# Cutting the stores behind a stream of loads into rows that grow from 4 KB to 64 KB

## The chip, the cores and the metric

The kernel runs on one core of a Trainium2 chip. The metric is the device time of one execution in microseconds (us). All timed executions here are in the fast state or, for single looks, of unknown state on one core at a granted clock of 1.0.

## The reference

Two inputs of 1024 x 4096 float32; the result is the GELU, in its tanh form, of their product.

```python
def reference(x, y):
    z = x * y
    return (0.5 * z * (1 + np.tanh(np.sqrt(2 / np.pi) * (z + 0.044715 * z ** 3)))).astype(np.float32)
```

## The kernel before

Each of 128 partitions holds 32,768 elements (128 KB) of x. x stays in SBUF (the memory on which the multiply and the GELU work; the inputs and the result lie in HBM, where the page has 33.55 MB read and 16.78 MB written), y goes through a ring of 64 KB; product and GELU are written over x in place, and x is stored. The loads and stores all go through the sync engine's one DMA queue (the page's only one, q1, with all 50.33 MB). Below, what the change and the argument touch (cuts marked by `# ...`).

```python
X_LOADS = [(0, 16384), (16384, 32768)]
Y_LOADS = [(0, 16384, 0), (16384, 24576, 0), (24576, 32768, 8192)]
STEP = 4096
STORES = [(0, 16384), (16384, 32768)]
# ...
    _hoist(nc, [load_x(0).ins, load_y(0).ins])     # issued first of all
    load_x(1)
    for i in (1, 2):
        nc.sync.wait_ge(sem_mul, (Y_LOADS[i][1] - Y_LOADS[1][0]) // STEP)
        load_y(i)
# ... vector: 8 multiplies of 128 x 4096; scalar: 8 GELUs of 128 x 4096, one behind each
    for i, (a, b) in enumerate(STORES):
        nc.sync.wait_ge(sem_act, b // STEP)
        nc.sync.dma_start(out=out_r[:, a:b], in_=xs[:, a:b]).then_inc(sem_o[i], 16)
    for i in range(len(STORES)):
        nc.sync.wait_ge(sem_o[i], 16)
```

The order on the queue is x, y, x (64 KB rows, 8.39 MB each), y, y (32 KB rows, 4.19 MB each), store, store (64 KB rows, 8.39 MB each). Of a 128-partition transfer each of the 16 DMA engines carries 8 rows, then one 4-byte packet for the semaphore: for the 7 transfers the trace has 896 packets of a row and 112 of 4 bytes, 1,008 in all.

Of the kernel before, what the change touches and what calls it, by code (L numbers as in the profile page):

```python
# [1 line left out]

# [4 lines left out]


F32 = mybir.dt.float32
GELU = mybir.ActivationFunctionType.Gelu_apprx_tanh  # L10


X_LOADS = [(0, 16384), (16384, 32768)]

Y_LOADS = [(0, 16384, 0), (16384, 24576, 0), (24576, 32768, 8192)]
STEP = 4096
STORES = [(0, 16384), (16384, 32768)]
Y_RING = 16384


def _hoist(nc, issued):

    here = nc.cur_bb.bb.instructions
    first = nc.main_func.blocks[0].instructions
    for ins in issued:
        del here[next(k for k, i in enumerate(here) if i is ins or i.name == ins.name)]
    engine = issued[0].engine
    at = next(
        k
        for k, i in enumerate(first)  # L30
        if i.engine == engine and type(i).__name__ == "InstDrain"
    )
    first[at:at] = issued


@with_exitstack
def kernel(
    ctx: ExitStack,
    tc: tile.TileContext,
    x: bass.AP,  # L40
    y: bass.AP,
    out: bass.AP,
):
    nc = tc.nc
    P = nc.NUM_PARTITIONS

    x_r = x.flatten_outer_dims().rearrange("(p a) c -> p (a c)", p=P)
    y_r = y.flatten_outer_dims().rearrange("(p a) c -> p (a c)", p=P)
    out_r = out.flatten_outer_dims().rearrange("(p a) c -> p (a c)", p=P)
    total_f = x_r.shape[1]  # L50


    tc.close()
    tc.compile()  # L54

    xs = nc.alloc_sbuf_tensor("xs", [P, total_f], F32).ap()
    ys = nc.alloc_sbuf_tensor("ys", [P, Y_RING], F32).ap()
    sem_x = [nc.alloc_semaphore(f"sem_x{i}") for i in range(len(X_LOADS))]
    sem_y = [nc.alloc_semaphore(f"sem_y{i}") for i in range(len(Y_LOADS))]
    sem_o = [nc.alloc_semaphore(f"sem_o{i}") for i in range(len(STORES))]  # L60
    sem_mul = nc.alloc_semaphore("sem_mul")
    sem_act = nc.alloc_semaphore("sem_act")

    def load_x(i):
        a, b = X_LOADS[i]
        return nc.sync.dma_start(out=xs[:, a:b], in_=x_r[:, a:b]).then_inc(sem_x[i], 16)  # L66

    def load_y(i):
        a, b, r = Y_LOADS[i]
        return nc.sync.dma_start(  # L70
            out=ys[:, r : r + b - a], in_=y_r[:, a:b]
        ).then_inc(sem_y[i], 16)

    _hoist(nc, [load_x(0).ins, load_y(0).ins])
# [5 lines that stand above are left out]
    n = 0  # L80
    for i, (a, b, r) in enumerate(Y_LOADS):
        for j, (xa, xb) in enumerate(X_LOADS):
            if xa <= a < xb:
                nc.vector.wait_ge(sem_x[j], 16)
        nc.vector.wait_ge(sem_y[i], 16)  # L85
        for c in range(a, b, STEP):
            nc.vector.tensor_mul(  # L87
                out=xs[:, c : c + STEP],
                in0=xs[:, c : c + STEP],
                in1=ys[:, r + c - a : r + c - a + STEP],  # L90
            ).then_inc(sem_mul, 1)
            n += 1
            nc.scalar.wait_ge(sem_mul, n)
            nc.scalar.activation(  # L94
                out=xs[:, c : c + STEP], in_=xs[:, c : c + STEP], func=GELU
            ).then_inc(sem_act, 1)

    for i, (a, b) in enumerate(STORES):
        nc.sync.wait_ge(sem_act, b // STEP)
        nc.sync.dma_start(out=out_r[:, a:b], in_=xs[:, a:b]).then_inc(sem_o[i], 16)  # L100
    for i in range(len(STORES)):
        nc.sync.wait_ge(sem_o[i], 16)
    nums = sorted(s.num for s in [*sem_x, *sem_y, *sem_o, sem_mul, sem_act])
    assert nums == list(range(nums[0], nums[-1] + 1))
    nc.sync.sem_clear(range(nums[0], nums[-1] + 1))


# [1 line left out]
_INS = ['x', 'y']  # L109
_OUTS = [((1024, 4096), 'float32')]  # L110


# [23 lines left out]
```

## Time and profile before

| | before |
|---|---|
| time, median of 3 runs | 121.03 us (120.79 to 121.08) |
| span in the profile | 119.5 us |
| DMA queue occupied | 98.5% |
| vector / scalar engine busy | 29% / 25% |
| last load of y, landing to landing | 10.4 us (its equal before it: 9.7) |

The prediction below quotes the lines. A transfer counts as landed at the last of its 16 semaphore updates (in this trace an update comes 0.28 to 0.39 us behind its engine's last packet). How to read the lines: the profile gives no row for a transfer as such. It gives the moment at which the sync engine issued it and the time from issue to landing, so the landing is their sum. On one queue that is never empty (98.5% occupied here), the time that a transfer itself took is the difference of its landing and that of the one ahead of it, not its time to landing.

In the text I also use two things that the trace records for each engine: the start and length of each packet (one row is one packet), and the 16 semaphore updates of each transfer, one for each engine. The "turn" is the place on the queue where a store follows a load. "Lost" is time beyond the full pace. From packets it is summed row by row. From landings it is the mean of the 16 updates of a transfer, less the same mean of the transfer ahead, less 9.71 us, which is what 4.19 MB in 32 KB rows took undisturbed (experiment 1; 9.72 us for the last load but one of the kernel before).

### The profile page before, as it was taken

How to read it: one execution, taken by the hardware profiler on the slowest of the kernel's cores; microseconds unless marked ns; L12 is line 12 of the kernel's file. 1: busy time of each engine (PE TensorE's matmuls, PEld its weight loads, DVE VectorE, ACT ScalarE, POOL GpSimd, SP SyncE). 2: the span in 40 equal slices, each digit the busy share in tenths (PEclk: the TensorE clock that was granted, in tenths of full speed). 3: DMA queues.
4: the chain of work that ended last, by engine and by line, in shares of the span. 5: the costliest groups of instructions: out<-in, count | busy, mean ns of one | idle time of the engine just before them, and what ended most of it. 6: DMA issues, size and time to landing. Idle time of an engine off the chain costs nothing.

```text
span 119.5 us, 68 instructions
## 1 busy us (share of the span) xinstructions
DVE 35.0 (29%) x8; ACT 30.2 (25%) x9; POOL 0.2 (0%) x4
## 2 busy tenths in 40 slices
DVE  0000000000000199999600049959990000000000
ACT  3000000000000006797780000977479200000000
POOL 0000000000000000000000000000000000000000
DMA  9889888998899889988898989998899888988890
GB/s 351 351 373 680 351 351 351 636 417 351 351 636 417 351 351 526 526 351 351 351 526 351 504 373 482 395 526 351 351 395 658 351 351 351 702 351 351 351 680 22
DMA packets 1008, 50.33 MB, mean 421 GB/s; under 512 B 112, under 2 KB 112, under 8 KB 112
## 3 DMA queue, kind: packets, MB, share of 16 engines
q1 hardware_dynamic: 1008, 50.33, 98.5%
HBM read 33.55 MB, written 16.78 MB: 421 GB/s over the span
## 4 chain that ended last, share of the span: by engine, by line
DMA 53%; DVE 22%; ACT 3%; SPq 0%; issue 0%; DVEq 0%
DMA ys<-in_y_dram 53%; DVE xs L87 22%; ACT xs L94 3%; SPq L66 0%; DVEq L85 0%
## 5 line engine op out<-in xcount | busy, mean ns | idle before, releaser
L87 DVE TENSOR_TENSOR xs<-xs,ys 128x4096 f32<-128x4096 f32 x8 | 35.0, 4421 | 54.7 <-DMA ys<-in_y_dram 54.7
L94 ACT ACTIVATE xs<-xs 128x4096 f32<-128x4096 f32 x8 | 28.9, 3617 | 61.1 <-DVE xs L87 61.1
L94 ACT ACT_TABLE_LOAD x1 | 1.3, 1283 | 1.9 <-PEq L54 1.9
L120 POOL MEMSET const-bfloat16-1.0<- 128x1 bf16 x1 | 0.1, 102 | 0.0
L120 POOL MEMSET const-uint8-127<- 128x1 uint8 x1 | 0.1, 102 | 0.0
L120 POOL MEMSET const-float32-1.0<- 128x1 f32 x1 | 0.1, 99 | 0.0
L120 POOL MEMSET const-float32-0.0<- 128x1 f32 x1 | 0.1, 98 | 0.2 <-issue 0.2
## 6 DMA issues: line engine op xcount, KB each, us to landing
ys<-in_y_dram SPq DMA_DIRECT2D x2, 4096.0 KB, 21.1
xs<-in_x_dram SPq DMA_DIRECT2D x2, 40.3
out_dram<-xs SPq DMA_DIRECT2D x2, 31.9
ys<-in_y_dram SPq DMA_DIRECT2D x1, 40.8
```

Of the source, the lines that this page charges most:

```text
L87: nc.vector.tensor_mul(out=xs[:, c : c + STEP], in0=xs[:, c : c + STEP], in1=ys[:, r + c - a : r + c - a + STEP],).then_inc(sem_mul, 1)
L94: nc.scalar.activation(out=xs[:, c : c + STEP], in_=xs[:, c : c + STEP], func=GELU).then_inc(sem_act, 1)
L120: nc = _bacc.Bacc("TRN2", target_bir_lowering=False, num_devices=1)
```

## The change

Its intent: the last load of y takes 0.7 us longer than its equal, and it is the one with a store queued behind it. The stores of the first half start in small rows and double, so that only a little store data stands right behind the loads.

```diff
-STORES = [(0, 16384), (16384, 32768)]
+STORES = [
+    (0, 1024),
+    (1024, 2048),
+    (2048, 4096),
+    (4096, 8192),
+    (8192, 16384),
+    (16384, 32768),
+]
@@
     for i, (a, b) in enumerate(STORES):
-        nc.sync.wait_ge(sem_act, b // STEP)
+        nc.sync.wait_ge(sem_act, -(-b // STEP))
         nc.sync.dma_start(out=out_r[:, a:b], in_=xs[:, a:b]).then_inc(sem_o[i], 16)
```

The rows of the six stores have 4, 4, 8, 16, 32 and 64 KB.

## The prediction

The sum 121.03 - 0.4 + 0.16, with a little more off for the case that the loss goes nearly whole, came to 120.7 us. Its 121.03 us are measured, and its 0.16 us are an estimate from measured prices (32 rows x 4.4 ns, 4 semaphores x 6 ns). The 0.4 stands as the bare estimate of how much of the measured 0.71 us would come back. "My theory" says no more than this: with small store rows behind it, the last load loses less. "Reading side" and "writing side" are to be read as the source and the destination of the transfers; the traces show no parts of an engine.

> **What bounds the kernel now.** I read the page's busy table and queue line first, to see which resource is full. In these lines the columns are: engine, busy us, share of the span, instructions; then the mean busy share of the DMA engines in 40 slices; then the one queue with its packets, MB and share of time.
>
> ```profile
> span 119.5 us, 68 instructions
> DVE 35.0 (29%) x8; ACT 30.2 (25%) x9; POOL 0.2 (0%) x4
> DMA  9889888998899889988898989998899888988890
> q1 hardware_dynamic: 1008, 50.33, 98.5%
> HBM read 33.55 MB, written 16.78 MB: 421 GB/s over the span
> ```
>
> The reader is to see that the two compute engines work a quarter of the span each, while the 16 DMA engines are occupied for 98.5% of it and no slice but the last is idle. The kernel is a stream of 50.33 MB through 16 engines. What matters is only whether an engine moves bytes in every moment.
>
> Second, the issues and landings of each tensor, from the views of one tile (ys, then xs, then the output), and the sync engine's waits:
>
> ```profile
> L70 SPq DMA_DIRECT2D ys<-in_y_dram x3: 328/328/433, 0.4 to 58.8; - x3
> DMA to landing us min/median/max: 20.2/22.0/40.8
> ```
>
> ```profile
> L66 SPq DMA_DIRECT2D xs<-in_x_dram x2: 328/357/386, 0.0 to 1.9; - x2
> DMA to landing us min/median/max: 21.9/31.9/58.7
> ```
>
> ```profile
> L100 SPq DMA_DIRECT2D out_dram<-xs x2: 343/346/348, 62.4 to 93.3; - x2
> DMA to landing us min/median/max: 26.1/31.9/37.7
> ```
>
> ```profile
> SPq L100 <- ACT xs L94: 33.8, 2, 30.5
> SPq L102 <- DMA out_dram<-xs: 25.8, 1, 25.8
> ```
>
> And the end of the chain of waits (start us, us, what):
>
> ```profile
> 58.80 21.99 DMA ys<-in_y_dram
> ...
> 89.68 3.62 ACT xs L94
> ```
>
> Adding issue time and time to landing gives the moment at which each transfer is complete, and the differences give what each took on the queue, since all share one queue and each was issued well before the one in front of it had ended:
> - x first half: 0.0 + 21.9 = 21.9. y first half: 0.4 + 40.8 = 41.2, so 19.3 for 8.39 MB. x second half: 1.9 + 58.7 = 60.6, so 19.4.
> - y third quarter: issued 50.1, 50.1 + 20.2 = 70.3, so 9.7 for 4.19 MB. y last quarter: 58.8 + 22.0 = 80.8, so 10.5 for the same 4.19 MB.
> - first store: 62.4 + 37.7 = 100.1, so 19.3 for 8.39 MB. second store: 93.3 + 26.1 = 119.4, so 19.3.
>
> Two readings carry the argument. The chain of waits names the multiply and the GELU, but the second store was issued at 93.3, 6.8 us before the queue was free of the first (100.1). So the compute and the waits of the sync engine are not on the path: the queue is never empty. And one transfer is odd: the last load took about 0.7 us more than its equal before it. It is the one with a store queued behind it.
>
> The single packet records of the trace sharpen this. A 64 KB row takes one engine 2,414 ns from its start to the next one's start, a 32 KB row 1,209.4 ns. Each engine's packets follow one another from 1.0 to 1.7 us until 118.6 to 119.1 us without gaps. Against this pace the time lost, mean of the 16 engines, is: 0.71 us on the first row of all[...], 0.03 us in the rest of the first 45 us, 0.16 us between 45 and 66 us, and 0.71 us (0.59 to 0.82) in the last two rows of the last load; nothing in all of the stores. In the engine that ends last, the last load's rows take 1,210 ns six times, then 1,828 and 1,266; the first 64 KB row of the store then takes 2,414 ns, as all store rows do. So the stall lies before the first store row[...]. Semaphore packets cost 6 ns each.
>
> [...]16 x 65,536 bytes in 2,414 ns is 434.4 GB/s; [...]2 x 1,209.4 - 2,414.4 = 4.4 ns for one more row. [...]The first two new stores have 0.5 MiB[...]; but here all are queued behind others, and no boundary between like transfers shows a loss in the trace beyond the 6 ns of the semaphore.
>
> **The change part by part.** Loads, multiplies and activations are untouched, in size and order. On the sync engine two stores become six; four issues of about 0.35 us are added. After the last load is issued (58.8) the waits for one and two activations have long been met (the activations end at 49.4 and 53.8), so the first four stores go out by about 60.5; the fifth waits for the fourth activation (62.4) as the first does now, and the last goes out at about 93.3 as now. The last load isn't off the queue before 80.8, so the earlier issue wins nothing, and the 0.35 us of each issue is hidden.
>
> On each DMA engine the store has 8 rows of each DMA: 16 rows before, 48 after, with the same bytes. So 32 more rows x 4.4 ns = 0.14 us, and 4 more semaphore packets x 6 ns = 0.02 us. Together +0.16 us on the path, if rows of 4 to 16 KB carry the same fixed cost as those of 32 KB, which no record here shows.
>
> What it is after is the 0.71 us. [...]0.71 us at 27.1 GB/s is 19 KB. [...]I estimate that between 0.2 and 0.6 of the 0.71 us comes back, 0.4 in the middle. Sum: -0.4 + 0.16, and a little more off for the case that it returns nearly whole; about -0.3 us. 121.03 - 0.3 = 120.7.
>
> **The rivals.**
> 1. The stall is a fixed price of turning from reading HBM to writing it (or from writing SBUF to reading it), whatever the rows. For it: all 16 engines pay a similar 0.6 to 0.8 us, close to the 0.71 us at the very start[...]. Against it: it lies up to 3 us ahead of the first store row, mostly in the last load row but one[...]. It would leave the stall and add the 0.16: 121.2.
> 2. Small rows are dearer than 4.4 ns each[...]. For it: a 4 KB row is done in 151 ns, shorter than the 0.35 us or so between an engine's last packet and its semaphore update in the trace. Against it: packets overlap by 3 to 4 ns in the records[...]. If 16 rows of 4 KB ran at half pace it would cost 16 x 151 ns = 2.4 us; at nine tenths 0.27 us. It would make the time 121.1 to 123.
> 3. The theory holds and the stall goes whole: 121.03 - 0.71 + 0.16 = 120.5.
> 4. The earlier issue of stores helps or blocks the queue: seven transfers would be outstanding at about 62 us in place of three. [...]no change of time.
>
> **Range and chances.** The floor of the change is 0.71 us, 0.6% of 121.03; even with all start-up losses gone as well a win of 2% (2.42 us) isn't there. A loss of 2% needs rival 2 at half pace. I give my theory with a part back 40%, rival 3 25%, rival 1 25%, rival 2 10%. The three runs before spread by 0.3 us. Predicted 120.7 us, 120.2 to 121.4 in eight of ten cases; faster by over 2% 1%, within 2% 97%, slower by over 2% 2%.
>
> **What would show it.** The last load's time from landing to landing should fall from 10.5 toward 9.7 to 10.1 us; if it stays at 10.5, rival 1 is right. The five stores of the first half should together take 19.4 to 19.6 us; well over 19.6 means rival 2. The last store should keep 19.3. DVE and ACT rows must be the same to 1%. The prediction would be wrong if the first stores ran at a visibly lower rate, if the stall moved to a later boundary between row sizes (4 to 8, 8 to 16 KB and so on), or if the multiply or activation were slowed by stores that read SBUF beside them.

## More of the kernel before

"The kernel before" is the kernel as it was before the change. The first eight experiments ran on one chip, where it had a median of 120.9 us, the last four on another, where it had 120.87; no trace of it was taken on that second chip.

## The result, and the profile after

| | before | changed |
|---|---|---|
| time, median of 6 runs each | 120.95 us (120.79 to 121.08) | 121.05 us (120.89 to 121.29) |
| ratio of fast runs | | 1.0009, 95% interval 0.9996 to 1.0023 |

A ratio is the mean time of one kernel's fast runs over that of the other's of the same rounds, so it is not quite the ratio of the medians. A second series of the changed kernel gave 1.0010 (0.9997 to 1.0024). The profile of the changed kernel, first the page (busy table, DMA occupancy in 40 slices, queue):

```profile
span 120.0 us, 74 instructions
DVE 35.0 (29%) x8; ACT 30.2 (25%) x9; POOL 0.2 (0%) x4
DMA  9899888988898889988999999989999999988890
q1 hardware_dynamic: 1584, 50.33, 98.5%
HBM read 33.55 MB, written 16.78 MB: 420 GB/s over the span
```

The same bytes go in 1,584 packets in place of 1,008: 576 more, or 36 for each of 16 engines: 32 rows and 4 semaphores. Nothing else moved. The loads of y and the stores of the changed kernel (issue times, then time to landing), the end of its chain of waits, and the store lines of its page (count, KB each, us to landing):

```profile
L77 SPq DMA_DIRECT2D ys<-in_y_dram x3: 328/328/433, 0.4 to 58.9; - x3
DMA to landing us min/median/max: 20.2/22.1/40.9
```

```profile
58.93 22.11 DMA ys<-in_y_dram
```

```profile
L107 SPq DMA_DIRECT2D out_dram<-xs x6: 332/444/473, 59.3 to 93.6; - x6
DMA to landing us min/median/max: 23.0/26.0/38.0
```

```profile
out_dram<-xs SPq DMA_DIRECT2D x1, 4096.0 KB, 38.0
...
out_dram<-xs SPq DMA_DIRECT2D x1, 26.3
```

The last load of y lands at 58.93 + 22.11 = 81.04. The one ahead of it was issued at 50.26 and took 20.2, so it landed at 70.45; the difference is 10.6 us, and not the 9.7 to 10.1 that I wanted to see. The fifth store was issued at 62.58 and lands at 62.58 + 38.0 = 100.6, so the first half was stored in 19.5 us against 19.3 before, and the last store, issued at 93.57, lands at 119.87, after 19.3 us as before. So the rows cost what was expected, and the stall is still there.

### The profile page after: what moved, and what is told of

Read it like the earlier page. It is cut to its first block, busy times and chain, and to the rows that moved or that the text cites. A ratio compares the mean times of both kernels' runs of the same rounds, so it can differ in the third digit from the quotient of the medians.

```text
span 120.0 us, 74 instructions
## 1 busy us (share of the span) xinstructions
DVE 35.0 (29%) x8; ACT 30.2 (25%) x9; POOL 0.2 (0%) x4
## 2 busy tenths in 40 slices
DMA packets 1584, 50.33 MB, mean 420 GB/s; under 512 B 176, under 2 KB 176, under 8 KB 432
## 3 DMA queue, kind: packets, MB, share of 16 engines
q1 hardware_dynamic: 1584, 50.33, 98.5%
## 4 chain that ended last, share of the span: by engine, by line
DMA 53%; DVE 22%; ACT 3%; SPq 0%; issue 0%; DVEq 0%
DMA ys<-in_y_dram 53%; DVE xs L94 22%; ACT xs L101 3%; SPq L73 0%; DVEq L92 0%
## 6 DMA issues: line engine op xcount, KB each, us to landing
ys<-in_y_dram SPq DMA_DIRECT2D x2, 4096.0 KB, 21.2
```

## The experiments

In the table, what each run lost at the turn from load to store, worked out from landings as said above (the mean of the engines). All but the two kernels themselves have one trace each:

| run | load ahead of the turn took, us | lost, us |
|---|---|---|
| before, first and second trace | 10.37, 10.47 | 0.66, 0.76 |
| changed, first and second trace | 10.56, 10.30 | 0.85, 0.59 |
| all stores in 4 KB rows | 10.49 | 0.78 |
| first stores in 512-byte rows | 10.22 | 0.51 |
| loads end in small rows | 10.92 | 1.1 |
| first store held back | 9.71 | 0.00 |
| SBUF copy between | 10.46 | 0.75, ahead of the copy |
| HBM copy between | 9.77 | 0.06, ahead of the copy |
| two turns | 10.50, then 19.41 for a store and a load | 0.79, then none (19.41 is 0.01 under twice 9.71) |
| two turns, dry between | 10.51, then see below | 0.80, then 1.14 |
| 8 KB of SBUF copy 40 us earlier | 10.13 | 0.05 ahead of the copy, 0.42 |
| 32 KB of SBUF copy 40 us earlier | 9.71 | 0.82 ahead of the copy, 0.00 |

Summed from the packets of the last rows, the kernel before lost 0.71 and 0.85 us in its two traces (mean 0.78) and the changed one 0.90 and 0.64 (0.77). So landings come out lower by 0.05 to 0.09 us, and for the 8 KB copy by more: 0.55 us from packets at the stores, where landings give 0.42.

I began with the theory of the prediction (the loss depends on the store rows behind the load, by their number; how an engine would bring that about no trace shows) and two rivals: a fixed price of the change of destination from SBUF to HBM, and a slow end of the load that has nothing to do with the store.

### 1. The first store held back

```diff
         nc.sync.wait_ge(sem_act, b // STEP)
+        if i == 0:
+            nc.sync.wait_ge(sem_y[2], 16)
```

> The kernel before, with the first store issued only once the last load has landed. What stalls the last two rows of the last load (0.71 us, mean of the engines)? If a store waiting behind them causes it (both my theory[...] and the rival, a price of the turn): the last load takes 9.7 us from landing to landing like its equal before it, with under 0.1 us lost in its last two rows, and instead the engines idle between load and store for 1.5 to 3 us; time 121.8 to 123.5. If the rows are slow for another reason (the multiply and GELU beside them, or the end of a load as such), the last load still takes 10.4 to 10.5 us, and the idle stretch comes on top.

Measured: 122.17 us (one run). The loads of y and the stores in its views:

```profile
L70 SPq DMA_DIRECT2D ys<-in_y_dram x3: 328/328/432, 0.4 to 59.3; - x3
DMA to landing us min/median/max: 20.2/21.2/41.3
```

```profile
L102 SPq DMA_DIRECT2D out_dram<-xs x2: 344/346/347, 80.6 to 93.0; - x2
```

The last load, issued at 59.3, lands after 21.2 us in place of 22.0, at 80.5. The one ahead of it landed at 50.6 + 20.2 = 70.8: 9.7 us. The packets lose 5 and 4 ns in its last two rows. From the end of its last row to the first store row the engines stand idle for 1.76 us. So a store that waits behind the load makes its last rows slow (0.66 and 0.76 us lost with it, 0.00 without); multiply and GELU ran beside both loads as before. Of the 1.3 us over the kernel before, some 0.4 lies in the first row of the program, long ahead of the edit: it lost 1.13 us in this run, and 0.57 to 0.81 in every other trace.

### 2. A copy from SBUF to SBUF between load and store

```diff
         nc.sync.wait_ge(sem_act, b // STEP)
+        if i == 0:
+            nc.sync.dma_start(out=cs[:, 0:3072], in_=xs[:, 0:3072]).then_inc(sem_c, 16)
```

> The kernel before with a copy from SBUF to SBUF (128 x 3072 f32, 12 KB rows, 1.57 MB, about 3.6 us of queue) between the last load and the first store; time about 121.0 + 3.6 = 124.7. If the stall belongs to the reading side's switch from HBM to SBUF[...]: 0.7 us lost in the last rows of the load, before the copy, and under 0.1 us at the copy's end, before the store. If it belongs to the writing side's switch from SBUF to HBM: nothing lost in the load's last rows and 0.7 us lost around the copy's end. If only the whole turn (both sides change) costs: neither, and the time is 0.7 us shorter, 124.0.

Measured: 124.47 us (one run). The end of its chain, the issue of the copy in order of time, and the copy's line on the page (KB, us to landing):

```profile
58.69 22.05 DMA ys<-in_y_dram
```

```profile
62.34 0.52 SPq L103 DMA_DIRECT2D cs<-xs  x1
```

```profile
cs<-xs SPq DMA_DIRECT2D x1, 1536.0 KB, 22.0
```

The load lands at 80.7, 10.5 us after the one ahead (50.02 + 20.2 = 70.2). The copy lands at 62.34 + 22.0 = 84.3, 3.6 us later, its full pace; no row of the copy, and none of the stores behind it, loses more than the 4 ns of a row. So the load stalls (0.75 us) ahead of a copy that writes no HBM at all, and the change from writing SBUF to writing HBM behind the copy cost nothing beyond those 4 ns. The rival of the destination has fallen: what changes where the load stalls is the source, from HBM to SBUF.

### 3. A copy from HBM to HBM between load and store

```diff
+        if i == 0:
+            nc.sync.dma_start(out=cd[:, 0:8192], in_=x_r[:, 0:8192]).then_inc(sem_c, 16)
```

> The kernel before with a copy from HBM to HBM (x's first 8192 columns to a scratch tensor, 32 KB rows, 4.19 MB, about 9.7 us of queue if it keeps the pace) between the last load and the first store. Mirror of the SBUF copy: if the stall belongs to the reading side's switch from HBM to SBUF: nothing lost in the last rows of the load, 0.6 to 0.8 us lost in the last rows of the copy, before the store. If it belongs to the writing side's switch from SBUF to HBM: 0.7 us in the last rows of the load, nothing in the copy's last rows. Time about 130.7 if the copy runs at full pace; more if a copy that both reads and writes HBM is slower.

Measured: 132.83 us (one run). The end of its chain, and its copy on the page:

```profile
58.74 21.65 DMA ys<-in_y_dram
```

```profile
copy_dram<-in_x_dram SPq DMA_DIRECT2D x1, 4096.0 KB, 30.4
```

The load lands at 80.39, 9.8 us after the one ahead (50.07 + 20.6 = 70.6), and its last two rows lose 2 ns each. So writing HBM behind the load did not stall it (0.06 us by landings). The second half of the expectation is only half met: the copy itself is slow, 12.1 us (mean of the engines) for what a load moves in 9.7. Its last two rows lose 0.60 and 0.50 us against 0.35 to 0.45 in the three ahead of them (15 of the 16 engines, in the packets of one the order could not be told apart). That is 0.2 to 0.4 us more in these two rows together than the pace of the rows ahead of them, less than the 0.6 to 0.8 foretold and mixed with the copy's own slowness: a stall at its end is not shown.

### 4. The loads end in small rows

```diff
-Y_LOADS = [(0, 16384, 0), (16384, 24576, 0), (24576, 32768, 8192)]
+Y_LOADS = [(0, 16384, 0), (16384, 24576, 0), (24576, 28672, 8192),
+           (28672, 30720, 12288), (30720, 31744, 14336), (31744, 32768, 15360)]
```

(The last two multiplies wait for the pieces that they read.) The text has two cases: the first figures for a stall tied to a number of rows, the second for one that is not.

> The kernel before with the last load cut into rows of 16, 8, 4 and 4 KB (the mirror of the change), stores as before with 64 KB rows. 24 rows and 3 semaphores more: +0.11 us. [...]the stall shrinks from 0.71 to under 0.3 us and sits in the last two or three 4 KB rows; time 120.5 to 120.8. [...]the stall stays at 0.6 to 0.9 us and begins 2 to 3 us before the store, that is in the 8 KB rows or first 4 KB rows; time 121.0 to 121.2.

Measured: 121.02 us (4 runs), ratio 1.0003 (0.9986 to 1.002). The four pieces took 10.92 us; less 9.71 and less 0.12 for rows and semaphores, 1.1 us were lost, more than the 0.6 to 0.9 foretold and than in any trace with load rows of 32 KB but the one of experiment 9; why is open. Nearly all of it lies in the first eight of the sixteen 4 KB rows (about 31, 91, 49, 139, 117, 250, 286 and 150 ns, with some doubt as to which row of an engine is which, and then 4 or 5 in most of the last eight), from 77.0 to 79.3 us, with the first store row at 80.6. So the stall isn't tied to the last two rows: it begins some 3.6 us ahead of the store and is over 1.3 us, or eight 4 KB rows, ahead of it. That two or three rows set it, the step on which my 0.4 us rested, has fallen. It had only looked like "the last two rows", because the rows had 32 KB there.

### 5 and 6. The two kernels once more

No edit: each kernel as it is, for a second trace.

> The changed kernel once more, for a narrower interval and a second trace. If the first trace is typical: ratio 1.000 to 1.002 of the kernel before, 0.8 to 1.0 us lost in the last two rows of the last load, 0.15 us for the extra rows and semaphores. If the stall was by chance long in the first trace (that was the slowest of its six runs) and the small rows do help: 0.3 to 0.6 us in the last load and a ratio under 0.999.

> The kernel before against itself, to see how far the stall and the time change from run to run. Ratio 1.000 within 0.002; 0.6 to 0.9 us lost in the last two rows of the last load, nothing in the stores. If it comes out near 0.9 as with the changed kernel, the difference of 0.2 us between the two traces is no effect of the rows.

Measured: the changed kernel 121.14 us (6 runs), ratio 1.0010 (0.9997 to 1.0024); the kernel before against itself 120.97 us (4 runs), ratio 1.0007 (0.9988 to 1.0025). The stall came out as 0.76 us in the kernel before and 0.59 in the changed one, the other way round than in the first traces (0.66 and 0.85). The means of two traces are 0.71 and 0.72. So the change doesn't move the stall as far as two traces can tell, and a single trace can't tell 0.2 us. The timed runs set the limit: the interval of the first series is 0.05 us faster to 0.28 us slower; less 0.17 us for rows and semaphores (experiment 7), at most 0.22 us of the stall can have come back. The expectation of 0.8 to 1.0 for the changed kernel was a miss of that kind.

### 7. All stores in 4 KB rows

```diff
-STORES = [(0, 16384), (16384, 32768)]
+STORES = [(a, a + 1024) for a in range(0, 32768, 1024)]
```

> All stores in 4 KB rows: 32 stores of 512 KB. 240 rows more for each engine at 4.4 ns (a 4 KB row took 155.3 ns in the changed kernel, 150.9 at the full pace) is 1.06 us, 30 semaphores at 6 ns 0.18 us: 122.1 to 122.3 with the stall as it is, 121.5 if 4 KB rows throughout took the stall away. If many small rows are dearer than their single price (rival 2), over 122.6.

Measured: 122.18 us (4 runs), ratio 1.0101 (1.0086 to 1.0116), or 1.22 us over 120.9. The estimate was 1.24. The stores in its view, the length of an issue in ns (min/median/max) among them:

```profile
L100 SPq DMA_DIRECT2D out_dram<-xs x32: 433/1150/8408, 59.1 to 106.9; - x32
```

The sync engine was held up in single issues for as long as 8.4 us, but no gap shows in the queue: every group of eight 4 KB rows loses 35 ns, 4.4 ns a row, from first to last. So the price of rows is right and simply adds up, and rival 2 (dear small rows) has fallen. By the same price the changed kernel's 32 rows and 4 semaphores cost 0.17 us; its trace has that very difference (19.51 us for the first half of the stores against 19.34, mean landings), though the timed runs, at 0.1 us, can't tell it from zero.

### 8. Two turns

```diff
-STORES = [(0, 16384), (16384, 32768)]
+STORES = [(0, 8192), (8192, 16384), (16384, 24576), (24576, 32768)]
@@
     for i in (1, 2):
+        if i == 2:
+            store(0)            # the first store goes ahead of the last load
         nc.sync.wait_ge(sem_mul, (Y_LOADS[i][1] - Y_LOADS[1][0]) // STEP)
         load_y(i)
```

> The suspected cost doubled: the kernel before with its stores cut in four of 32 KB rows, and the first of them issued ahead of the last load, so that the queue goes load, store, load, store. 16 store rows and 2 semaphores more: +0.08 us. If the cost belongs to the reading side's switch from HBM to SBUF alone: two stalls of 0.7 to 0.9 us, each in the last rows of the load ahead of a store, and nothing at the switch back; time 121.6 to 121.9. If each switch, back too, costs 0.7 us: 122.3 to 122.6. If the cost isn't one of the switch: one stall, 121.0 to 121.1.

Measured: 121.18 us (4 runs), ratio 1.0015 (1.0000 to 1.0030). The loads of y, and the end of the chain:

```profile
L70 SPq DMA_DIRECT2D ys<-in_y_dram x3: 328/328/424, 0.4 to 58.8; - x3
DMA to landing us min/median/max: 21.0/31.8/40.8
```

```profile
58.81 31.79 DMA ys<-in_y_dram
```

The load ahead of the first store now took 21.0 us to land where it took 20.2 before: the stall has moved to it, at a time (66 to 71 us) when neither the multiply nor, past 62.4 us, the GELU was at work. From its landing (71.1) to that of the last load (90.6) a store and a load took 19.5 us, twice 9.7: nothing was lost at the turn back, nor at the second turn from load to store (the last two rows lose 36 ns or less). The count is that of the third expectation, one stall, and neither of the two that I had reasons for: the cost was paid at the first turn (0.79 us) and not again. By the ratio the run is 0.18 us (0.00 to 0.36) over the kernel before; 0.08 us of it are the price of rows and semaphores, and the rest is within the interval.

This made me form a new theory: the loss is paid once, for as long as the queue stays full, and anew once it has run dry.

### 9. Two turns, with a dry queue between

```diff
         if i == 2:
             store(0)
+            nc.sync.wait_ge(sem_o[0], 16)
```

(The first case is that of the new theory.)

> The kernel with two turns, where the second turn cost 0.03 us instead of 0.7, with the last load now issued only when the store ahead of it has landed, so that the engines run dry between that store and the load. [...]the second turn stalls again: 0.6 to 0.9 us in the last rows of the last load; time 121.2 + 0.7 + a dry stretch of about 2.5 us, 124 to 125. Rival: the stall comes once in a program, or only where the first store meets the loads: the second turn loses under 0.1 us again; 123.3 to 124.

Measured: 124.64 us (one run). The chain of its waits, from the store to the last load:

```profile
53.80 26.98 DMA out_dram<-xs
...
80.79 13.29 DMA ys<-in_y_dram
```

The same last load takes 13.3 us from its issue. The engines are dry for 1.9 us, its first row loses 0.49 us (the first row of the program lost 0.57 to 0.81, in experiment 1 1.13), and its last two rows lose 0.16 and 0.99 us, where without the dry stretch they lost 0.03. The stall is back: it is not paid once for a program. Here it was paid anew after the queue had run dry and a load came first.

### 10 and 11. A little SBUF reading, 40 us earlier

A copy of zeros from one small SBUF buffer to another goes between y's first load and x's second, with C = 256 (1 KB rows) or C = 1024 (4 KB rows).

```diff
+    nc.gpsimd.memset(cs, 0.0).then_inc(sem_m, 1)
+    nc.sync.wait_ge(sem_m, 1)
+    nc.sync.dma_start(out=cd, in_=cs).then_inc(sem_c, 16)      # [128, C] float32
     load_x(1)
```

The first case of each text is that of the new theory: what is lost at the copy grows with its bytes, and is not lost again at the first store.

> The kernel before with a small copy from SBUF to SBUF (128 x 256 f32, eight 1 KB rows for each engine, 8 KB) between y's first half and x's second half, 40 us ahead of the stores. It adds 0.30 us of bytes and 0.04 of rows. [...]it can be no longer than the 8 KB take, 0.30 us, in the rows before the copy; and [...]the turn at the first store loses so much less (0.4 to 0.6 us); 121.2 to 121.4. If a switch has a fixed price: 0.7 us before the copy; and 0.7 us at the first store too if it is paid each time (122.0).

> The same with 4 KB rows (128 x 1024 f32, 32 KB for each engine, 1.21 us). [...]0.6 to 0.9 us lost before the copy, under 0.2 us at the first store; time 121.0 + 1.25 = 122.2 to 122.4. If each turn pays: 0.7 us at both, 122.9 to 123.1. If the stall needs a store to HBM behind it: nothing before the copy, 0.7 us at the store.

Measured: 120.99 us with 8 KB for each engine, 122.31 with 32 KB (single runs). The loads of y with 32 KB, and the end of its chain:

```profile
L74 SPq DMA_DIRECT2D ys<-in_y_dram x3: 327/328/425, 0.4 to 59.7; - x3
DMA to landing us min/median/max: 21.4/22.5/41.8
```

```profile
59.74 22.50 DMA ys<-in_y_dram
```

The first load of y takes 41.8 us to land in place of 40.8: the last row ahead of the copy loses 0.87 us. At the turn to the stores, 40 us later, nothing is lost: the last load lands at 82.24, the one ahead of it at 51.07 + 21.4 = 72.5, so 9.7 us. The stores themselves are the kernel's own. With 8 KB only 0.05 us are lost ahead of the copy and 0.42 at the stores (0.55 from packets, too near to the 0.64 of one trace of the changed kernel to be called a saving). So the amount grew with the SBUF bytes that stood behind the load, from 0.05 us at 8 KB to 0.82 at 32 KB (landings), and is no fixed price; and with 32 KB what was paid early wasn't paid again (0.00 us at the stores). There's no gain in it: the 32 KB copy adds its own 1.2 us, by an estimate from its bytes at the 2,414 ns of a 64 KB row. The 8 KB copy, by the same estimate with its rows and semaphore 0.34 us on the queue, leaves 120.99 beside a median of 120.87, below the 121.2 to 121.4 foretold; whether a smaller one could gain was not tried.

### 12. First stores in 512-byte rows

```diff
+STORES = [(a, a + 128) for a in range(0, 2048, 128)] + [(2048, 16384), (16384, 32768)]
```

The second case is that of the prediction: a number of rows, here some tens, sets the stall.

> The change pushed further: the first 2048 columns are stored in sixteen stores of 512-byte rows (64 KB for each engine), then rows of 56 and 64 KB. 128 rows more at 4.4 ns and 15 semaphores: +0.65 us, so 121.6 to 121.7 with the stall as it is. [...]the stall shrinks to 0.1 to 0.5 us; 121.1 to 121.5. If 512-byte rows are dearer than 4.4 ns over their bytes: above 121.8, seen in the rows themselves.

Measured: 121.22 us (4 runs), ratio 1.003 (1.0013 to 1.0046), 0.36 us (0.16 to 0.56) over the kernel before where the price of rows and semaphores alone is put at 0.65. The stall was 0.51 us, lower than in any other trace with a store queued behind a load and no copy ahead, but by only 0.08. The time, which is under that price, and the stall both speak for it, though one trace does not show it, that with rows as small as this, or with as few bytes behind the load, some of the stall goes, but less than the rows cost. Which of the two it would be stays open: the sync engine could not issue all sixteen stores in time:

```profile
L100 SPq DMA_DIRECT2D out_dram<-xs x18: 332/468/8421, 59.0 to 93.0; - x18
```

Its eighth store took 8.4 us to issue and the ninth 6.1, so that at 77 us only about nine of them, 36 KB for each engine, stood behind the load.

## Why the prediction was right or wrong

- **Full DMA queue, compute off the path:** right. Every effect found is one of the queue (98.5% occupied in both profiles); the multiply and GELU rows are the same in number and length (8 of 4.42 us and 8 of 3.62 us in both).
- **The place of the loss:** right in that it comes from a store behind the load (experiment 1: 0.00 us without it) and from a change of the source to SBUF (2 and 3: 0.75 us ahead of a copy from SBUF, 0.06 ahead of one from HBM). Wrong in the detail "the last two rows": it is a stretch from about 3.6 to 1.3 us ahead of the store (4).
- **0.4 of the 0.71 us comes back with small rows:** this step failed. In place of 0.4 us, 0.0 came back (0.71 against 0.72 us from landings, 0.78 against 0.77 from packets, means of two traces each). Its ground was a limit of a few rows that was not shown: the stall isn't set by a count of a few rows, for 4 KB rows throughout left 0.78 us. No line of the profile had said that rows are what counts: it had only one row size on each side of the turn, and I read two rows of 32 KB as a number of rows.
- **Price of the rows, +0.16 us:** right, 0.17 us in the trace, and 1.22 for an estimated 1.24 when scaled up (7).
- **Hidden issues:** right. The first five stores were issued from 59.3 to 62.9, 18 us ahead of their turn.
- **The rivals:** the first, that the stall stays whatever the rows, gave 121.2 and is the nearest single figure to what came (121.05). But its reason, a fixed price of each turn, is wrong too: the second turn was free (8: 0.03 us), the loss came back after a dry queue (9: 1.14 us) and grew with bytes (10, 11: 0.05 us with 8 KB, 0.82 with 32 KB). So the sign "if it stays at 10.5, rival 1 is right" did not hold: the load took 10.6 us and rival 1's reason is still wrong. The second fell (7, for rows of 4 KB), the third didn't happen, the fourth was right for the change.
- **The sum:** 121.03 - 0.4 + 0.16, a little more off, was put at 120.7; without the failed term it is 121.2. The range held the result because it had been drawn to hold rival 1; for the theory itself that is luck. The time is the same, since the gain never came about and the price is 0.14% of the time.

What is shown: the loss came where, on a queue full of loads, the source changes from HBM to SBUF (0.75 us ahead of the copy from SBUF, 0.06 ahead of that from HBM); it was paid at the first turn (0.79 us), not at the second (0.03), and again once the queue had run dry (1.14); store rows of 4 to 64 KB made no difference that these runs can tell (0.59 to 0.85 us). What in an engine brings it about is not shown: the trace has one record for each packet and nothing of what goes on inside. What also stays open is why the stall varies between 0.59 and 0.85 us from trace to trace, and whether it comes too when the stores go through a queue other than that of the loads, which was not tried.

## What to carry to other kernels

On a full queue, find the loss first in differences of landings of equal transfers, and ask by experiment what it depends on before you shape rows for it: here one run with all stores in 4 KB rows (0.78 us still lost) would have shown that row size wasn't the lever, and a held-back store and two copies with one side changed what is. Here the first turn from loads to stores on the queue cost 0.59 to 0.85 us (mean of the engines, load rows of 32 KB, store rows of 4 to 64 KB), the second 0.03 us with the queue full and 1.14 us after a dry stretch; a wait that drains the queue to "separate" the two took away the stall and still made the run longer (by 1.3 us in experiment 1, some 0.4 of it from that run's slow first row). Splitting stores cost little here, 4.4 ns a row for each engine (1.22 us for 240 rows and 30 semaphores more), so split where it lets work start earlier, and not where all of it is queued behind other work anyway.
